# Which of two sequences goes first: the sample through projections, attention and recurrence before the prompt, and the feed-forward begun with the sample

## The chip, the cores and the metric

The kernel runs on one core of one Trainium2 chip. TensorE (PE in the rows) multiplies matrices into PSUM banks, VectorE (DVE), ScalarE (ACT) and GpSimd (POOL) do the elementwise work, and every DMA is issued from SyncE's queue (SP). The metric is the device time of one execution in microseconds (us), as a median over runs. For one execution there is a profile: start and duration of each instruction, and what ended each wait.

## The reference

One encoder layer is applied to two token sequences with the same weights: the prompt ("p", 512 tokens) and the sample ("s", 1024 tokens), 1024 features each.

```python
mod = (jax.nn.silu(c) @ w_ada + b_ada)[:, None, :]
sh1, sc1, g1, sh2, sc2, g2 = jnp.split(mod, N_MOD, axis=-1)
n = rms_norm(x, ln1_g) * (1 + sc1) + sh1
z = n @ w_in
q, k, v, xl, gl = jnp.split(z, [D_ATT, 2 * D_ATT, 3 * D_ATT, 3 * D_ATT + D_LRU], axis=-1)
...
att = neighbourhood_attention(q, k, v, rpb)
xl = depthwise_conv(xl, lru_conv_w, lru_conv_b)
h = (rg_lru_direction(xl, w_r_f, b_r_f, w_i_f, b_i_f, lam_f, False)
     + rg_lru_direction(xl, w_r_b, b_r_b, w_i_b, b_i_b, lam_b, True))
lru = (h * jax.nn.gelu(gl.astype(jnp.float32))).astype(x.dtype)
mix = jnp.concatenate([att, lru], axis=-1) @ w_out
x = x + g1 * mix
n2 = rms_norm(x, ln2_g) * (1 + sc2) + sh2
up = depthwise_conv(n2 @ w_up, ffn_conv_w, ffn_conv_b)
ug, uv = jnp.split(up, 2, axis=-1)
x = x + g2 * ((jax.nn.gelu(ug) * uv) @ w_down)
```

The feed-forward is 1024 to 2 x 2816 and back, in 22 blocks h of 128 hidden features. Everything is fp32. A product is made as three matmuls of rounded parts (hi x hi, hi x lo, lo x hi), so each operand is first split into two parts by elementwise instructions.

## The kernel before, in words

The program is written as a list of operations: `Recorder.op` notes each operation's cost estimate, what it reads and writes, and its buffers, and issues nothing. `Recorder.run` then makes a plan on the host. It gives each operation a due time (from the place in the list and from what depends on it) and goes through the engines in the order of that plan, with room in two SBUF arenas (F and R, whose border moves at each `turn`) and eight PSUM banks as conditions. Operations with two possible engines (a split's copy on ACT or DVE, a difference on DVE or POOL) get theirs there. The result is one fixed order of instructions for each engine. On the chip each engine follows its order, and waits for what the next instruction needs.

Where the plan leaves PE without work for over 900 ns it puts in filler, matmuls of the identity into an empty bank (`spin`), 128 columns wide in fp32. They are made in two passes, and so have two records each in the trace. The rule is:

```python
IDLE, SHARE = 900.0, 0.6
...
            if e == "PE" and s - done > IDLE:

                k = int(SHARE * (s - done) / 221.0)
                ...
                    events.append(lambda k=k, at=min(free, key=lambda x: emptied[x]): self.spin(at, k))
```

Filler is executed whether or not PE would have to wait there on the chip.

The stages, in the order of the list before the change:

- Start: four chunks of the modulation matrix, the prompt's first norm, weights.
- For j = 0 to 3 the prompt's heads 2j and 2j+1 and one quarter of the recurrence (`proj`: `qkv`, `mod_chunk`, `lru`), then the same for the sample (j = 3 to 0). Beside each `proj`, `weave` puts the attention (`attend`) of the step ahead of it. The sample's norm stands ahead of its first `proj`.
- The last attention (sample, j = 0) goes beside the loading of w_out and the prompt's output projection (`out_proj`), which leaves x2 = x + g1 * mix in DRAM.
- The sample's two output projections of 512 tokens, beside the second norm (`norm2`) of the prompt and of the sample's first half. `norm2` reads x2 back, normalizes and transposes it, and `a_terms` makes from its quarter blocks 11, 12, 21, 22 the four sums s1 to s4 and splits all: the seven left operands of a Strassen-Winograd product, which has seven products in place of eight (`WINO`).
- The first four feed-forward blocks for the prompt alone, as plain products (eight quarter products, `plain=True`), beside `norm2` of the sample's second half. Then blocks 4 to 21 for both by the seven products, and blocks 0 to 3 for the sample.
- The down projection, again by seven products (`DOWN`), reads the hidden features back from DRAM, in pairs of blocks, and ends with the last product over three groups of tiles.

In the rows, L376 is the emitting line that all recorded operations share, L497 the transposes and L323 the filler. Buffers appear by arena, not by purpose: arena_f and pieceNF are fp32 room, arena_r and pieceNR room for split operands.

Of the kernel before, what the change touches and what calls it, by code (L numbers as in the profile page):

```python
# [32 lines left out]
STEPS = (140, 134, 160, 176, 186, 96, 124)  # L33
# [13 lines left out]
ONLY_P = 4  # L47

BOOST = 2e4
# [785 lines left out]
def encoder(ctx: ExitStack, tc: tile.TileContext, x_p, x_s, c_t, ada, bada, bgate, lng, w_qkv, w_xg,  # L835
# [371 lines left out]

    def chain(*gens):
        for g in gens:
            for _ in g:  # L1210
                yield 1
            yield 1
# [51 lines left out]
    def norm2(q, g, xt):  # L1264
        norm_scale(xt)
        yield 1
        if q == "p":
            for f in (0, 2):
# [11 lines left out]
                if ONLY_P:  # L1280
                    keep("21", halved(full["21"], "n2x", None, [P, 2, 256]))
# [33 lines left out]
    xt = norm1_load("p", 0)  # L1315
    wq0, wx0, wg0 = [], [], []
    for ci in range(4):
# [14 lines left out]
        for f in (2 * ci, 2 * ci + 1):  # L1332
            norm_feature("p", 0, 1, xt, n1["p"], f)
# [28 lines left out]
    prev = w3 = wxg3 = None  # L1362

    for n, (q, j) in enumerate([("p", j) for j in range(4)] + [("s", j) for j in (3, 2, 1, 0)] + [("d", 0)]):
        out = []
        if q == "d":
            R.turn(1)
            main, nmain = chain(load_wo(), out_proj("p", [0])), 2
        else:
            if (q, j) == ("p", 3):  # L1370
                w3, wxg3 = load_w(w_qkv[j], 384), [load_w(w_xg[i + j], P) for i in (0, 4)]
            w, wxg = (wq0, (wx0, wg0)) if n == 0 else (w3, wxg3) if j == 3 else (None, None)
            main, nmain = proj(q, j, n + 4, out, w, wxg, n == 0), 6 if q == "p" else 13
            if n == 4:
                main, nmain = chain(norm_all("s"), main), 61
        if prev is None:
            weave(main, nmain, None, 1)
        else:
            pq, pj, pk = prev
            weave(main, nmain, attend(pq, pj, pk), 7 if pq == "p" else 15)  # L1380
        prev = (q, j, out[0]) if out else None
# [9 lines left out]

    R.turn(2)
    weave(out_proj("s", [0]), 4, norm2_of("p", 0), 2)
    R.turn(3)
    weave(out_proj("s", [1]), 8, norm2_of("s", 0), 7)
# [19 lines left out]
    def up(h, qs, plain=False):  # L1415
# [33 lines left out]
        if plain:  # L1449
            w = {k: halved(full[k], "wu", None) for k in ("11", "21", "12", "22")}  # L1450
            for q in qs:
                th = seqs[q]["T"] // 2
                for n in range(2):
                    pt = R.bank("up")
                    for m in range(2):
# [38 lines left out]
    def ups(hs, qs, plain):  # L1494
        for h in hs:
            up(h, qs, plain)
            if h == ONLY_P - 1:
                R.turn(4)
# [226 lines left out]
```

## Time and profile before

| | us |
|---|---|
| median of 2 runs | 1711.74 (1709.38 to 1714.09) |
| the profiled execution | 1708.56 |
| span of its instructions | 1706.8 |
| PE busy | 1664.3 (98%) |
| PE weight loads (PEld) | 1419.9 (83%) |
| DVE, ACT, POOL busy | 1344.4, 826.0, 550.8 |

The profiled execution lies 3.2 us below the median, and its span 1.8 us below its own time. A busy PE counts the filler as work, and its matmuls overlap, so that two neighbours that each last 0.39 us start 0.23 us apart. What PE loses in a stretch is therefore read as its idle time there plus the busy time of the filler.

### The profile page before, as it was taken

The numbers are of one execution on the slowest core, as the hardware profiler recorded it, in microseconds if no ns is written. First come the engines' busy times: TensorE is split into PE (matmuls) and PEld (weight loads), VectorE is DVE, ScalarE is ACT, GpSimd is POOL, SyncE is SP. The second block draws the span as 40 slices with busy tenths as digits, with TensorE's granted clock in tenths as the row PEclk, the third lists the DMA queues.
The fourth block names the chain that finished last, engine by engine and source line by source line (L and its number), as shares of the span: only waits on it lengthen the run. The fifth ranks groups of instructions, "written<-read, shape, count | busy, mean of one in ns | idle before, by whom it ended". The sixth has DMA issues, their size and how long they took to land.

```text
span 1706.8 us, 25295 instructions
## 1 busy us (share of the span) xinstructions
PE 1664.3 (98%) x9098; PEld 1419.9 (83%) x9098; DVE 1344.4 (79%) x2501; ACT 826.0 (48%) x1433; POOL 550.8 (32%) x344
## 2 busy tenths in 40 slices
PE   8999899999998999999999999999999999999898
PEld 6888697879886888998888888888888888888687
DVE  6898986978799957687777767677778777987896
ACT  3678955767877724554343333334346432232130
POOL 0242220211226205173322222222136210595593
PEclk9999999999998999999999999999999999999999
DMA  9665242524356383631321121212122478657861
GB/s 368 238 219 179 75 166 81 207 84 157 134 199 236 115 264 121 231 118 38 93 66 59 56 75 56 73 52 81 46 76 90 134 249 304 236 178 241 274 219 62
DMA packets 130477, 253.90 MB, mean 149 GB/s; under 512 B 13600, under 2 KB 45984, under 8 KB 130352
## 3 DMA queue, kind: packets, MB, share of 16 engines
q1 hardware_dynamic: 130352, 252.29, 44.1%
q8 instruction: 71, 1.16, 0.3%
q14 instruction: 54, 0.44, 0.1%
HBM read 207.66 MB, written 44.58 MB: 148 GB/s over the span
## 4 chain that ended last, share of the span: by engine, by line
PE 69%; DVE 9%; DMA 6%; ACT 6%; POOL 5%; issue 4%; SPq 1%; DVEq 0%; ACTq 0%; POOLq 0%
PE bank L376 67%; DVE arena_f L376 2%; POOL arena_r L376 2%; PE bank L497 2%; DVE arena_r L376 2%; ACT arena_f L376 2%; ACT piece3F L376 1%; DVE piece3F L376 1%; DVE piece4F L376 1%; ACT L376 1%; POOL arena_f L376 1%; SPq L376 1%; DMA piece3F<-in_ada_dram 1%; DMA piece4F<-in_gatew_dram 1%; ACT piece4F L376 1%
## 5 line engine op out<-in xcount | busy, mean ns | idle before, releaser
L376 PE MATMUL bank<-arena_r 128*128 128x512 f32 (+3 forms) x2700 | 653.6, 366 | 10.7 <-DVE piece4F L376 4.1
L376 PEld LDWEIGHTS bank<-arena_r 128*128 128x128 f32 (+1 forms) x2700 | 480.9, 189 | 90.3 <-DVE piece4F L376 5.0
L376 POOL TENSOR_TENSOR arena_f<-arena_f 128x512 f32<-128x512 f32 (+1 forms) x83 | 117.1, 1413 | 366.5 <-DMA arena_f<-in_w_up_dram 115.3
L376 PE MATMUL bank<-arena_r,piece5R 128*128 128x256 f32 (+1 forms) x1028 | 227.9, 323 | 2.3 <-DVE arena_f L376 1.1
L376 PE MATMUL bank<-piece0R,arena_r 128*128 128x512 f32 (+2 forms) x683 | 210.2, 391 | 2.1 <-ACT piece3F L376 1.4
L376 PEld LDWEIGHTS bank<-arena_r,piece5R 128*128 128x128 f32 x1028 | 168.5, 189 | 23.1 <-DVE piece5R L376 2.1
L376 PE MATMUL bank<-arena_r,piece0R 128*128 128x384 f32 (+3 forms) x750 | 179.3, 345 | 2.8 <-DVE piece0R L376 2.0
L376 DVE SCALAR_TENSOR_TENSOR arena_f<-bank,arena_s,arena_f 128x511 f32<-128x511 f32 (+3 forms) x306 | 153.8, 534 | 23.1 <-ACT arena_f L376 16.0
L376 PE MATMUL bank<-arena_r,piece3R 128*128 128x256 f32 (+1 forms) x686 | 163.1, 328 | 1.1 <-DVE bank L376 0.7
L376 ACT ACTIVATE arena_f<-arena_f,arena_s 128x384 f32<-128x384 f32 (+3 forms) x183 | 110.9, 616 | 95.1 <-DVE arena_f L376 65.6
L376 POOL TENSOR_TENSOR arena_r<-arena_f,arena_r 128x768 fp32r<-128x768 f32 (+2 forms) x60 | 100.3, 1681 | 154.2 <-ACT arena_r L376 53.4
L376 PEld LDWEIGHTS bank<-piece0R,arena_r 128*128 128x128 f32 (+1 forms) x683 | 123.1, 188 | 29.6 <-ACT piece3F L376 2.4
L376 PEld LDWEIGHTS bank<-arena_r,piece0R 128*128 128x128 f32 (+1 forms) x750 | 129.8, 189 | 13.6 <-issue 4.4
L376 ACT ACTIVATE arena_f<-bank 128x512 f32<-128x512 f32 (+2 forms) x149 | 69.2, 470 | 137.2 <-DVE bank L376 77.3
L376 ACT ACTIVATE arena_f<-bank,arena_s 128x512 f32<-128x512 f32 (+1 forms) x134 | 91.2, 689 | 84.5 <-PE bank L376 62.4
L376 PEld LDWEIGHTS bank<-arena_r,piece3R 128*128 128x128 f32 x686 | 116.2, 189 | 15.3 <-DVE bank L376 0.9
L376 ACT ACTIVATE arena_r<-arena_f 128x768 fp32r<-128x768 f32 (+3 forms) x97 | 69.2, 720 | 86.6 <-PE bank L376 43.9
L376 DVE TENSOR_TENSOR arena_r<-arena_f,arena_r 128x768 fp32r<-128x768 f32 (+2 forms) x79 | 84.2, 1074 | 5.8 <-ACT arena_r L376 4.7
L376 DVE TENSOR_TENSOR arena_f<-arena_f 128x512 f32<-128x512 f32 (+2 forms) x78 | 73.3, 950 | 13.6 <-ACT arena_f L376 12.5
L376 ACT ACT_TABLE_LOAD x53 | 68.0, 1283 | 11.1 <-issue 4.7
L376 PE MATMUL bank<-piece0R,piece3R 128*128 128x512 f32 (+1 forms) x227 | 69.0, 373 | 0.0
L376 DVE TENSOR_TENSOR bank<-bank,arena_f 128x512 f32<-128x512 f32 (+1 forms) x80 | 46.1, 576 | 25.5 <-PE bank L376 14.1
(454 smaller groups left out, 3131.8 us busy)
## 6 DMA issues: line engine op xcount, KB each, us to landing
arena_f<-in_w_up_dram SPq DMA_DIRECT2D x98, 256.0 KB, 3.5
arena_f<-gd SPq DMA_DIRECT2D x55, 384.0 KB, 3.8
gd<-arena_f SPq DMA_DIRECT2D x62, 256.0 KB, 3.3
arena_f<-in_bias_s_dram SPq DMA_DIRECT2D x31, 384.0 KB, 5.5
arena_f<-in_w_qkv_dram SPq DMA_DIRECT2D x28, 384.0 KB, 5.4
piece4F<-in_ada_dram SPq DMA_DIRECT2D x18, 512.0 KB, 9.0
piece3F<-in_ada_dram SPq DMA_DIRECT2D x16, 512.0 KB, 8.1
piece1F<-in_w_down_dram SPq DMA_DIRECT2D x31, 256.0 KB, 5.1
```

The lines of the kernel that those rows point to most:

```text
L376: fn(**{k: (v.real() if isinstance(v, View) else v) for k, v in kw.items()})
L497: self.op("PE", 107.0, lambda: self.nc.tensor.transpose(out.real(), in_.real(), ident.real()), [in_, ident], [out])
```

## The change

The sample now goes through the first norm, the projections, attention and the recurrence ahead of the prompt. The second half of its tokens is normalized right ahead of the loop. The prompt follows (j = 3 to 0). w_out is loaded beside the second of the prompt's steps. The sample's first output projection goes beside the prompt's last `proj`, its second one and `norm2` of its first half beside the prompt's last attention. Then come the prompt's output projection beside `norm2` of the sample's second half, the first two feed-forward blocks (h = 0, 1) for the sample alone by the seven products, beside `norm2` of the prompt, then blocks 2 to 21 for both, and blocks 0 and 1 for the prompt. The plain form is gone, and so is the extra split term that it needed. The borders of the arenas (`STEPS`) and one constant of the due times (`BOOST`) have other values. `mixed` interleaves two parts in a given proportion.

```diff
-STEPS = (140, 134, 160, 176, 186, 96, 124)
+STEPS = (146, 160, 174, 172, 182, 98, 130)
...
-ONLY_P = 4
-
-BOOST = 2e4
+ONLY = 2
+WO = 5
+
+BOOST = 16e3
...
+    def mixed(a, na, b, nb):
+
+        i = j = 0
+        while a is not None or b is not None:
+            if b is None or (a is not None and i * nb <= j * na):
+                i += 1
+                if next(a, 0) == 0:
+                    a = None
+                    continue
+            else:
+                j += 1
+                if next(b, 0) == 0:
+                    b = None
+                    continue
+            yield 1
...
-                if ONLY_P:
-                    keep("21", halved(full["21"], "n2x", None, [P, 2, 256]))
...
-    xt = norm1_load("p", 0)
+    xt = norm1_load("s", 0)
...
-            norm_feature("p", 0, 1, xt, n1["p"], f)
+            norm_feature("s", 0, 1, xt, n1["s"], f)
...
-    for n, (q, j) in enumerate([("p", j) for j in range(4)] + [("s", j) for j in (3, 2, 1, 0)] + [("d", 0)]):
-        out = []
-        if q == "d":
-            R.turn(1)
-            main, nmain = chain(load_wo(), out_proj("p", [0])), 2
-        else:
-            if (q, j) == ("p", 3):
...
+    norm_group("s", 1, 1, norm1_load("s", 1), n1["s"])
+
+    for n, (q, j) in enumerate([("s", j) for j in range(4)] + [("p", j) for j in (3, 2, 1, 0)] + [("d", 0)]):
+        out = []
+        if q == "d":
+            R.turn(1)
+            main, nmain = mixed(out_proj("s", [1]), 4, norm2_of("s", 0), 10), 14
+        else:
+            if (q, j) == ("s", 3):
...
+            if n == 4:
+                main, nmain = chain(norm_all("p"), main), 9
+            elif n == WO:
+                main, nmain = chain(load_wo(), main), 15
+            elif n == 7:
+                main, nmain = mixed(main, 6, out_proj("s", [0]), 4), 10
...
     R.turn(2)
-    weave(out_proj("s", [0]), 4, norm2_of("p", 0), 2)
+    weave(out_proj("p", [0]), 4, norm2_of("s", 1), 6)
     R.turn(3)
-    weave(out_proj("s", [1]), 8, norm2_of("s", 0), 7)
...
-    weave(ups(range(ONLY_P), ["p"], True), max(ONLY_P, 1), norm2_of("s", 1), 6)
+    weave(ups(range(ONLY), ["s"]), 7 * ONLY, norm2_of("p", 0), 4)
     R.turn(4)
...
-    for h in range(ONLY_P, NH):
-        up(h, ["p", "s"])
-    for h in range(ONLY_P):
-        up(h, ["s"])
+    for h in range(ONLY, NH):
+        for _ in up(h, ["p", "s"]):
+            pass
+    for h in range(ONLY):
+        for _ in up(h, ["p"]):
+            pass
...
-    pairs = list(range(ONLY_P // 2, NH // 2)) + list(range(ONLY_P // 2))
+    pairs = list(range(ONLY // 2, NH // 2)) + list(range(ONLY // 2))
```

Counted over both programs, PE has 2248 matmuls of 256 columns before and 2200 after. Those of 384 and of 512 columns are as many as before (1344 and 4482). Of 128 columns there are 652 and 820: the 544 transposes stay, and filler goes from 108 matmuls in 11 runs to 276 in 21 runs. The first run, at the start of the program, has 33 in both. After the change 42 stand in the eight runs from the prompt's first norm to its last projection, and 201 in the twelve runs from the prompt's output projection on. In the program the lines are shifted by one: L324, L377 and L498.

The first place is PE's order behind the transposes of `norm2` of the sample's second half. Before, the plain products of the prompt follow (256 columns wide, moving operand 256):

```order
L497 MATMUL bank_72<-ident,arena_f 128x128 x4
L323 MATMUL bank_67<-ident 128x128 x21
L376 MATMUL bank_74<-arena_r,piece0R 128x256 x12
L376 MATMUL bank_74<-piece3R 128x256 x6
L376 MATMUL bank_74<-arena_r,piece3R 128x256 x6
```

After, the third and the fourth tile of the prompt's output projection follow there (512 columns wide, two banks of 24 matmuls a tile):

```order
L498 MATMUL bank_73<-ident,arena_f 128x128
L498 MATMUL bank_73<-ident,piece5F 128x128
L324 MATMUL bank_72<-ident 128x128 x19
L377 MATMUL bank_74<-piece0R 128x512
...
L377 MATMUL bank_67<-arena_r,piece0R 128x512 x15
L324 MATMUL bank_72<-ident 128x128 x54
L377 MATMUL bank_74<-piece0R,arena_r 128x512
L377 MATMUL bank_74<-piece1R,arena_r 128x512
```

One run of 21 became two of 19 and 54, and 48 matmuls of 512 columns stand between them.

The second place is PE's order where `norm2` of the sequence that comes last is made: the sample's before, beside block 4 (and before it the plain products), the prompt's after, beside block 1. Before:

```order
L376 MATMUL bank_69<-piece1R,arena_r 128x512 x3
L323 MATMUL bank_67<-ident 128x128 x6
L376 MATMUL bank_68<-arena_r,piece5R 128x256 x7
...
L376 MATMUL bank_69<-piece0R,arena_r 128x512
L323 MATMUL bank_71<-ident 128x128 x8
L376 MATMUL bank_68<-arena_r,piece5R 128x256 x12
```

After, where block 1 is made for the sample alone:

```order
L377 MATMUL bank_71<-arena_r 128x512 x9
L324 MATMUL bank_69<-ident 128x128 x48
L377 MATMUL bank_71<-piece3R,arena_r 128x512 x3
L377 MATMUL bank_71<-piece0R,arena_r 128x512 x3
L377 MATMUL bank_71<-arena_r 128x512 x6
L324 MATMUL bank_69<-ident 128x128 x6
L377 MATMUL bank_74<-arena_r 128x512 x9
L377 MATMUL bank_74<-piece0R,arena_r 128x512 x3
L324 MATMUL bank_69<-ident 128x128 x10
```

Each of the last three products of block 1 (12 matmuls) has a run of filler ahead of it, of 48, 6 and 10, and a run of 18 follows ahead of block 2.

The third place is DVE's order around the split of the output projection's tiles. Before, the split's difference for the third tile of the sample's second half (1024 elements, into piece3R) stands between the evictions of the third and of the fourth tile of its first half, so that three tiles of matmuls lie ahead of the ones that need it:

```order
L376 TENSOR_TENSOR piece4F<-bank_74,arena_f 128x512
L376 TENSOR_TENSOR piece4F<-bank_73,arena_f 128x512
L376 TENSOR_TENSOR piece4F<-piece4F 128x1024
L376 TENSOR_TENSOR piece3R<-arena_f,piece3R 128x1024
L376 TENSOR_TENSOR piece4F<-bank_74,arena_f 128x512
```

After, for the prompt's fourth tile, the split's difference (the last row) stands behind the evictions of the third tile (the first three rows) and instructions of the sample's `a_terms`, so that none of the output projection's matmuls lie ahead any more:

```order
L377 TENSOR_TENSOR arena_f<-bank_74,arena_f 128x512
L377 TENSOR_TENSOR arena_f<-bank_67,arena_f 128x512
L377 TENSOR_TENSOR arena_f<-arena_f 128x1024
L377 TENSOR_TENSOR arena_f<-arena_f 128x512
L377 TENSOR_TENSOR piece0R<-arena_f,piece0R 128x512
L377 TENSOR_TENSOR arena_f<-arena_f 128x512
L377 TENSOR_TENSOR arena_r<-arena_f,arena_r 128x512
L377 TENSOR_TENSOR arena_f<-arena_f 128x512
L377 TENSOR_TENSOR arena_r<-arena_f,arena_r 128x512 x2
L377 TENSOR_TENSOR arena_f<-arena_f 128x512
L377 TENSOR_TENSOR arena_r<-arena_f,arena_r 128x512
L377 TENSOR_TENSOR arena_r<-arena_f,arena_r 128x1024
```

From the difference for the third tile to that for the fourth, DVE's order has in all 9 differences and 6 sums of 512 elements, the two evictions, the sum of 1024 elements, and the difference for the fourth tile itself.

## Rows read from the trace of the kernel before

**Rows 1.** The page: busy us, share of the span and records of each engine

```profile
PE 1664.3 (98%) x9098; PEld 1419.9 (83%) x9098; DVE 1344.4 (79%) x2501; ACT 826.0 (48%) x1433; POOL 550.8 (32%) x344
```

**Rows 2.** Stretches: length, busy PE, PEld, DVE, ACT, POOL, PE's granted clock, DMA, GB/s

```profile
0.00:60.00 60.00, 55.70 (x334) 40.79 (x335) 39.38 (x128) 23.68 (x39) 2.80 (x8) 0.97 0.95 360
180.00:240.00 60.00, 53.98 (x339) 47.86 (x337) 52.69 (x143) 44.31 (x79) 20.04 (x14) 0.97 0.27 91
525.00:560.00 35.00, 28.93 (x136) 21.35 (x135) 33.20 (x51) 32.28 (x49) 27.99 (x10) 0.80 0.57 190
715.00:760.00 45.00, 43.02 (x365) 42.82 (x364) 36.31 (x49) 25.19 (x40) 24.19 (x16) 1.00 0.44 139
780.00:830.00 50.00, 48.13 (x281) 41.82 (x280) 34.99 (x60) 18.85 (x33) 12.27 (x9) 1.00 0.17 48
```

**Rows 3.** The same stretches, busy PE and PEld of the filler (L323) alone

```profile
0.00:60.00 60.00, 10.02 (x66) 9.82 (x66) 0.97 0.95 360
180.00:240.00 60.00, 8.38 (x66) 7.96 (x66) 0.97 0.27 91
525.00:560.00 35.00, 2.08 (x8) 1.78 (x8) 0.80 0.57 190
715.00:760.00 45.00, 5.68 (x48) 5.53 (x48) 1.00 0.44 139
780.00:830.00 50.00, 3.44 (x28) 3.43 (x28) 1.00 0.17 48
```

**Rows 4.** The filler's run of 21 by itself

```profile
733.00:738.00 5.00, 4.78 (x42) 4.77 (x42) 1.00 0.71 188
```

**Rows 5.** Stretches of the feed-forward: up for both, its end, down, down's last product

```profile
830.00:1300.00 470.00, 469.90 (x2687) 412.70 (x2687) 352.19 (x649) 185.64 (x321) 113.80 (x84) 1.00 0.22 67
1300.00:1380.00 80.00, 78.25 (x341) 63.25 (x340) 61.78 (x95) 42.06 (x66) 33.33 (x23) 1.00 0.43 135
1380.00:1600.00 220.00, 220.00 (x972) 182.16 (x971) 176.73 (x197) 54.90 (x78) 98.16 (x56) 1.00 0.73 247
1600.00:1625.00 25.00, 18.96 (x72) 13.95 (x71) 23.27 (x20) 3.91 (x5) 25.00 (x14) 0.93 0.72 243
```

**Rows 6.** PE in order of time, 703 to 741: start, us, instruction, idle before

```profile
703.42 0.39 PE L376 MATMUL bank<-piece0R,arena_r 128*128 128x512 f32 x1
...
721.81 2.32 PE L376 MATMUL bank<-arena_r,piece4R 128*128 128x256 f32 x18
723.97 1.60 PE L376 MATMUL bank<-arena_r,piece3R 128*128 128x256 f32 x12
...
730.05 3.33 PE L497 MATMUL bank<-ident,arena_f 128*128 128x128 f32 x29
733.22 4.85 PE L323 MATMUL bank<-ident 128*128 128x128 f32 x42
...
740.29 1.46 PE L376 MATMUL bank<-arena_r,piece0R 128*128 128x256 f32 x10 [1.98 <-DVE piece0R L376]
```

**Rows 7.** POOL in order of time, 733 to 780: the first and the last

```profile
733.03 1.52 POOL L376 TENSOR_TENSOR arena_f<-arena_f 128x512 f32<-128x512 f32 x1 [44.00 <-PE bank L497]
...
778.21 1.67 POOL L376 TENSOR_TENSOR arena_r<-arena_f,arena_r 128x512 fp32r<-128x512 f32 x1 [2.25 <-DVE arena_r L376]
```

**Rows 8.** The stretches of `a_terms`: the sample's second half, the prompt

```profile
729.00:780.00 51.00, 49.02 (x374) 46.96 (x373) 46.76 (x42) 29.44 (x51) 41.81 (x26) 1.00 0.40 119
655.00:684.00 29.00, 29.00 (x146) 24.48 (x145) 27.38 (x21) 16.01 (x27) 23.69 (x14) 1.00 0.44 142
```

**Rows 9.** DVE's groups of one shape, whole span: busy us, mean ns, idle before

```profile
L376 DVE TENSOR_TENSOR arena_f<-arena_f 128x512 f32<-128x512 f32 x74 | 68.0, 930 | 13.2 <-ACT arena_f L376 12.5 <-POOL arena_f L376 0.6
L376 DVE TENSOR_TENSOR arena_r<-arena_f,arena_r 128x512 fp32r<-128x512 f32 x26 | 29.9, 1156 | 2.4 <-ACT arena_r L376 2.1
L376 DVE TENSOR_TENSOR arena_f<-bank,arena_f 128x512 f32<-128x512 f32 x26 | 17.8, 685 | 3.6 <-PE bank L376 3.5
```

**Rows 10.** DVE's groups in the stretch 520 to 800, 1024 elements

```profile
L376 DVE TENSOR_TENSOR arena_r<-arena_f,arena_r 128x1024 fp32r<-128x1024 f32 x2 | 2.4, 1220 | 0.8 <-ACT arena_r L376 0.8
```

More of the change, by code (lines that the diff above doesn't have):

```diff
@@ L1360, in encoder @@
     R.ts(spn8, acc, -8.0, None, ALU.mult)
-    prev = w3 = wxg3 = None
-    for n, (q, j) in enumerate([("p", j) for j in range(4)] + [("s", j) for j in (3, 2, 1, 0)] + [("d", 0)]):
-        out = []
-        if q == "d":
-            R.turn(1)
-            main, nmain = chain(load_wo(), out_proj("p", [0])), 2
-        else:
-            if (q, j) == ("p", 3):
[L1371 to L1381, printed above, removed]
     def norm2_of(q, g):
@@ L1390, in norm2_of @@
         yield from norm2(q, g, xt)
+    prev = w3 = wxg3 = None
+    norm_group("s", 1, 1, norm1_load("s", 1), n1["s"])
[6 more added lines that the diff above has]
+            if (q, j) == ("s", 3):
+                w3, wxg3 = load_w(w_qkv[j], 384), [load_w(w_xg[i + j], P) for i in (0, 4)]
+            w, wxg = (wq0, (wx0, wg0)) if n == 0 else (w3, wxg3) if j == 3 else (None, None)
+            main, nmain = proj(q, j, n + 4, out, w, wxg, n == 0), 6 if q == "p" else 13
+            if n == 4:
[4 more added lines that the diff above has]
+                main, nmain = mixed(main, 6, out_proj("s", [0]), 4), 10
+        if prev is None:
+            weave(main, nmain, None, 1)
+        else:
+            pq, pj, pk = prev
+            weave(main, nmain, attend(pq, pj, pk), 7 if pq == "p" else 15)
+        prev = (q, j, out[0]) if out else None
     R.turn(2)
-    weave(out_proj("s", [0]), 4, norm2_of("p", 0), 2)
+    weave(out_proj("p", [0]), 4, norm2_of("s", 1), 6)
     R.turn(3)
-    weave(out_proj("s", [1]), 8, norm2_of("s", 0), 7)
     def wu_blocks(h):
@@ L1413, in encoder, with up @@
     off = {"p": 0, "s": TP}
-    def up(h, qs, plain=False):
+    def up(h, qs):
         full = wu_blocks(h)
@@ L1447, in finish @@
                 R.dma(g_d[h, :, off[q] + i * 512:off[q] + i * 512 + 512], cu)
[L1449 to L1455, printed above, removed]
-                        sts = [tuple(v[:, k * P:k * P + P] for v in w["12"[kk] + "12"[n]]) for kk in range(2) for k in range(4)]
-                        R.mm3(pt[:, m * th:m * th + th], sts, [n2[q]["12"[m] + "12"[kk], k] for kk in range(2) for k in range(4)])
-                    centre(q, n, 0, pt)
-                    side(q, n, 0, pt)
-                finish(q)
-            return
         for name, ka, kb, bank, first in WINO:
@@ L1492, in up, with ups @@
                     finish(q)
-    def ups(hs, qs, plain):
+            yield 1
+    def ups(hs, qs):
         for h in hs:
-            up(h, qs, plain)
-            if h == ONLY_P - 1:
-                R.turn(4)
-            yield 1
-    weave(ups(range(ONLY_P), ["p"], True), max(ONLY_P, 1), norm2_of("s", 1), 6)
+            yield from up(h, qs)
+    weave(ups(range(ONLY), ["s"]), 7 * ONLY, norm2_of("p", 0), 4)
     R.turn(4)
```

## The prediction

> **What bounds the kernel now.** I read the page first, then stretches, then the order of time on PE and POOL at the seam between attention and feed-forward. PE is busy for 98% of the span, and no other engine over 79% [rows 1]. So the time is PE's work plus what PE loses. In the up stage PE is busy for 469.90 of 470 us, and in most of the down stage for all of it [rows 5]; there only the number of matmuls counts. But a busy PE includes filler. In the first 60 us it executes 10.02 us of filler and idles 4.30. Four later stretches hold all the other filler [rows 2, 3], and what they lose, idle time and filler together, is:
>
> - 180 to 240 (from the prompt's to the sample's projections): 6.02 + 8.38 = 14.40 us, 33 filler matmuls;
> - 525 to 560 (end of attention): 6.07 + 2.08 = 8.15 us, 4 of them;
> - 715 to 760 (`norm2` of the sample's second half): 1.98 + 5.68 = 7.66 us, 24 of them;
> - 780 to 830 (the first blocks for both): 1.87 + 3.44 = 5.31 us, 14 of them.
>
> Together 35.52 us for 75. The change is decided by what it does to these losses, and by how many matmuls there are.
>
> **Matmuls.** 48 of 256 columns go: four plain blocks for the prompt were 4 x 96 = 384, and as seven products they are 4 x 84 = 336. Between 721.81 and 723.97, 18 such matmuls start [rows 6], 0.120 us each. 48 x 0.120 = 5.8 us less, all on the path. Transposes and wide matmuls stay. That two blocks of feed-forward instead of four are made for one sequence at a time moves DVE and ACT work about; in the up stage DVE is busy for 352 of 470 us [rows 5], and its cover remains. I cost it at nothing.
>
> **Filler.** The orders show 276 filler matmuls instead of 108, with the first 33 in both. Their own price: 21 of them keep PE busy for 4.78 us [rows 4], 0.228 each. They are executed in any case, so 243 later ones cost at least 55.3 us. They stand where PE's next instruction was expected late, so waits come on top. The four stretches give a price with the waits: 35.52 / 75 = 0.474 us for one filler matmul, from 12.97 / 38 = 0.341 (715 to 760 and 780 to 830, beside `norm2` and `a_terms`) to 14.40 / 33 = 0.436 (180 to 240, where a new sequence's norm is made). The stretch with only four is dominated by something else: its clock was granted at 0.80 on average [rows 2]. So the bounds are:
>
> - low: 243 x 0.228 = 55.3 us, 19.8 more than the 35.5 of now;
> - high: 243 x 0.474 = 115.1 us, 79.6 more.
>
> I take the nearest stretch for each. The 42 before the prompt's output projection are like 180 to 240: 42 x 0.436 = 18.3 us. The 201 behind it are like the two stretches beside `a_terms`: 201 x 0.341 = 68.6 us. Together 86.9, which is 51.4 more than now.
>
> **Does the seam really wait that long?** Two chains say that there is something to wait for. First, the sample's second half. Its `a_terms` begin on POOL at 733.03 and end at 779.88, POOL almost without a break [rows 7], with DVE busy for 46.76 of 51 us [rows 8]. That is 47 us. Before, PE had the prompt's plain products beside it, whose operands were all there. After, the list leaves two tiles of the prompt's output projection, 96 matmuls of 512 columns. 972 of these take 220.00 us [rows 5], 0.226 each, so 21.7 us, which leaves 25 us open. And the second of these tiles isn't ready: on DVE the difference for its split stands behind 9 differences and 6 sums of 512 elements, two evictions and one sum of 1024. By [rows 9, 10] these and the difference itself take 9 x 1.156 + 6 x 0.930 + 2 x 0.685 + 2 x 1.22 = 19.8 us, while PE has one tile, 48 x 0.226 = 10.9 us. PE is short of some 9 us there, and executes 54 filler matmuls, 12.3 us.
>
> Second, the prompt. From the last output matmul at 703.42 to the block of transposes at 730.05 it takes 26.6 us now (eviction, x2 to DRAM and back, squares, scaling) [rows 6], and the prompt's `a_terms` lie in a stretch of 29 us [rows 8]. So some 56 us pass from the prompt's last output matmul to its last operand. Beside it PE has blocks 0 and 1 for the sample: 168 x 0.226 = 38.0 us. 18 us stay open, and the splits of block 1's own weights stand in the same queues. Both chains together leave PE 43 us short, against 45.8 us (201 x 0.228) of filler there. That is without contention between the two chains, which share DVE, POOL and ACT, so it speaks for the low end or more, and not for less.
>
> On the other hand the Trainium skill, "Perfetto Trace Analysis", section Optimization Strategy, says that a kernel whose busiest engine changes over time may gain from interleaving such regimes. By that rule sample-first would gain, since it puts output projection and feed-forward of one sequence beside the norms of the other. The trace shows such interleaving already before (POOL and DVE above 80% beside a PE at 96%, [rows 8]), so it decides no term here; it is the reason for the first rival below, which has its time from rows alone.
>
> **Start.** In the first 60 us the DMA engines are busy for 0.95 of the time at 360 GB/s [rows 2]. SP's order now has the sample's other four x tiles (4 x 0.5 MB) ahead of the fifth chunk of the modulation, which is 2.1 MB / 360 GB/s = 5.8 us if nothing covers it, and nothing if the projections of the first half do. DVE has a second norm there, beside 39.38 us of work in 60. I take 3 us, from 0 to 6.
>
> **The rest.** The end of attention, which lost 8.15 us [rows 2, 3], is the prompt's after the change, with tiles of the sample's output projection and one norm beside it; its loss is in the 35.5 and in the new price alike. The tail of the up stage (1.75 us idle) becomes the prompt's alone, and the down stage's last product idles 6.04 us with POOL busy throughout [rows 5]; its pairs of blocks are only rotated by one instead of two. I leave both as they are, plus or minus 4 us.
>
> **Sum.** -5.8 + 51.4 + 3 = +48.6 us on the profiled execution's 1708.56: **1757 us**, 2.6% above the median of 1711.74. About 2% (34 us, so 1746) is what a measurement of this kernel tells from no change.
>
> **Rivals.**
>
> 1. *The filler only fills.* The waits are as long as the filler and no longer: each chain ends while it runs, since the chains' 43 us and the filler's 45.8 agree. The loss is 55.3 us: -5.8 + 19.8 + 3 = +17.0, **1726 us**, 0.8% above the median and so not slower by the bound. It decides if PE's idle time in the seam is below some 5 us in all. For it: the run of 21 is followed by a wait of only 1.98 us [rows 6]. Against it: filler covers only 0.6 of a gap by its own rule, and all four stretches show idle time beside it.
> 2. *The clock falls in the gaps.* At 525 to 560 PE waited several times and its granted clock was 0.80 on average, so part of that stretch ran at 1.2 instead of 2.4 GHz; the loss was 8.15 us for four filler matmuls [rows 2, 3]. Six runs of 15 to 54 with waits behind them could each do that. All at 0.474: -5.8 + 79.6 + 3 = +76.8, **1785 us**. The Trainium skill, "TensorE: Matmul & The Clock Gate", section "Why this matters for your kernels", says that gaps between bursts of matmuls put the array back to half rate. Stretch 525 to 560 agrees; stretches 715 to 760 and 780 to 830 held the clock (granted 1.00) with filler.
> 3. *A real gain.* Even where nothing is lost in the later stretches but the filler itself, 55.3 us of filler stand against 35.5 lost now. With all idle time of the start (4.30), of the up stage's tail (1.75) and of the down stage's last product (6.04) gone as well, it is 1708.6 - 5.8 + 19.8 - 12.1 = **1710 us**, the same time.
>
> That the sample is begun with is in the order, so "it does not do what it says" is no case.
>
> **How the numbers follow.** Forecast (waits as at the nearest stretches, 1757): 0.50. Filler only (1726): 0.27. Clock (1785): 0.18. A real gain or something else: 0.05. The range goes from the filler-only case to the clock case with the start's and the end's few us: 1722 to 1788. Faster by over 2% (below 1677): 0.01. Within 2%: the filler-only case, a small part of the forecast's, and most of the rest, 0.33. Slower by over 2%: 0.66.
>
> **What would show it.** 552 records of L324 and some 62 us of PE busy on them, of which 46 us behind the start of the prompt's output projection; PE's idle time beside the later filler some 32 us (86.9 less 55.3); the up stage still without idle time; 0 to 60 us much as before. The forecast is wrong at its root if PE's idle time falls in spite of the filler, for then the places of the filler say nothing on waits; it is mis-sized if idle time beside the filler is below 10 us or above 50, or if the start or the down stage differ by more than 10 us.

## The result, and the profile after

The kernel after takes 1771.88 us (median of 2 runs, 1770.01 to 1773.74) against 1711.74: 1.0351 times as long, 95% interval 1.0319 to 1.0383. The profiled execution took 1773.74 us, its span is 1772.0, which is 65.2 us more than before. The forecast of 1757 us was 15 us short, inside its range.

The page of the kernel after, its line of engines, beside [rows 1]:

```profile
PE 1711.7 (97%) x9386; PEld 1459.8 (82%) x9386; DVE 1383.3 (78%) x2548; ACT 842.1 (48%) x1452; POOL 539.4 (30%) x327
```

PE is busy for 47 us longer although, filler apart, it has 48 matmuls less. Stretches of the kernel after, columns as in [rows 2]; all engines:

```profile
0.00:60.00 60.00, 54.20 (x350) 40.06 (x351) 38.76 (x138) 30.34 (x50) 0.96 (x7) 0.97 0.78 301
180.00:520.00 340.00, 327.75 (x1961) 281.69 (x1960) 294.13 (x735) 271.76 (x499) 99.11 (x58) 0.98 0.49 169
520.00:640.00 120.00, 119.86 (x615) 98.66 (x614) 82.02 (x188) 65.15 (x122) 15.15 (x8) 1.00 0.55 187
640.00:900.00 260.00, 238.64 (x1328) 204.95 (x1327) 166.61 (x258) 90.95 (x150) 71.40 (x46) 0.95 0.28 91
900.00:1300.00 400.00, 397.48 (x2264) 347.68 (x2263) 309.40 (x565) 149.94 (x252) 73.26 (x53) 1.00 0.20 61
1620.00:1665.00 45.00, 34.79 (x129) 26.67 (x128) 41.07 (x38) 13.06 (x19) 24.19 (x13) 0.81 0.74 242
```

The same of its filler alone (L324 in this kernel; here the column after the length is PE's):

```profile
0.00:60.00 60.00, 9.04 (x66) 0.97 0.78 301
180.00:520.00 340.00, 12.86 (x84) 0.98 0.49 169
640.00:900.00 260.00, 46.91 (x402) 0.95 0.28 91
```

And 640 to 900 us in the kernel before, first all engines, then (L323) the filler:

```profile
640.00:900.00 260.00, 256.05 (x1562) 228.29 (x1561) 200.67 (x297) 116.99 (x195) 100.33 (x64) 1.00 0.35 111
640.00:900.00 260.00, 9.13 (x76) 1.00 0.35 111
```

In both kernels 640 to 900 us holds the seam: `norm2`, its `a_terms`, and the first blocks of the feed-forward. What PE loses there, idle time and filler together, is 3.95 + 9.13 = 13.1 us before and 21.36 + 46.91 = 68.3 after, 55.2 more. The start loses 14.8 (14.3 before), and 520 to 640 nothing, where the end of attention stood [rows 2, 3].

How the seam loses is seen where the largest burst of `a_terms` lies. Before, that of the sample's second half, in steps of 10 us:

```profile
740.00:750.00 10.00, 9.71 (x81) 9.71 (x82) 10.00 (x10) 5.31 (x9) 9.40 (x6) 1.00 0.54 144
750.00:760.00 10.00, 10.00 (x86) 10.00 (x85) 9.79 (x10) 4.90 (x8) 9.09 (x7) 1.00 0.47 156
760.00:770.00 10.00, 10.00 (x73) 9.42 (x72) 10.00 (x11) 5.38 (x11) 10.00 (x7) 1.00 0.18 61
770.00:780.00 10.00, 10.00 (x57) 8.73 (x56) 9.36 (x8) 4.95 (x11) 7.62 (x5) 1.00 0.38 107
```

After, that of the prompt:

```profile
760.00:770.00 10.00, 8.92 (x55) 7.61 (x54) 10.00 (x10) 8.15 (x15) 7.97 (x6) 1.00 0.46 136
770.00:780.00 10.00, 10.00 (x92) 10.00 (x91) 10.00 (x9) 5.16 (x9) 10.00 (x7) 1.00 0.56 150
780.00:790.00 10.00, 5.30 (x19) 3.88 (x18) 6.59 (x6) 1.52 (x3) 4.81 (x3) 0.83 0.24 74
790.00:800.00 10.00, 8.29 (x50) 6.67 (x49) 5.91 (x11) 1.59 (x2) 0.00 (x0) 0.98 0.01 2
```

Both have DVE and POOL at or near 10 of 10 us while the burst lasts. Before, PE has the prompt's plain quarters beside that. After, its work has run out, as PE in order of time shows (start, us, instruction, idle before); the rows of 699 and 714 are the same story at the sample's second half:

```profile
699.24 12.22 PE L324 MATMUL bank<-ident 128*128 128x128 f32 x108
714.60 0.80 PE L377 MATMUL bank<-piece0R,arena_r 128*128 128x512 f32 x1 [3.14 <-ACT arena_r L377]
...
769.73 10.88 PE L324 MATMUL bank<-ident 128*128 128x128 f32 x96
781.57 0.73 PE L377 MATMUL bank<-piece3R,arena_r 128*128 128x512 f32 x2 [0.96 <-ACT arena_r L377]
786.04 0.79 PE L377 MATMUL bank<-piece3R,arena_r 128*128 128x512 f32 x1 [3.74 <-DVE arena_r L377]
```

12 and 11 us of filler, each with waits for a split operand behind it. And as soon as the burst is over, POOL has nothing to do (0.00 in the row from 790, and in each 10 us up to 830): the elementwise work is not too much for the whole seam (DVE 166.61 of 260 us, less than before), it is too much at once.

### The profile page after: what moved, and what is told of

Its sections match the earlier page's. It is cut to its first block, busy times and chain, and to the rows that moved or that the text cites. A ratio compares the mean times of both kernels' runs of the same rounds, so it can differ in the third digit from the quotient of the medians.

```text
span 1772.0 us, 25907 instructions
## 1 busy us (share of the span) xinstructions
PE 1711.7 (97%) x9386; PEld 1459.8 (82%) x9386; DVE 1383.3 (78%) x2548; ACT 842.1 (48%) x1452; POOL 539.4 (30%) x327
## 4 chain that ended last, share of the span: by engine, by line
PE 51%; DVE 9%; DMA 2%; ACT 1%; issue 1%; POOL 1%; SPq 0%; ACTq 0%; DVEq 0%; POOLq 0%
PE bank L377 51%; DVE arena_f L377 4%; DVE arena_r L377 2%; ACT arena_f L377 1%; DVE piece5F L377 1%; DVE piece5R L377 1%; DMA arena_f<-catdp 0%; PE bank L498 0%; DMA x2ds<-arena_f 0%; DMA piece4F<-in_w_down_dram 0%; DVE piece4F L377 0%; POOL arena_r L377 0%; DVE piece0R L377 0%; DVE piece0F L377 0%; DVE piece2F L377 0%
## 5 line engine op out<-in xcount | busy, mean ns | idle before, releaser
L377 PE MATMUL bank<-arena_r 128*128 128x512 f32 (+2 forms) x2916 | 709.4, 371 | 13.2 <-POOL arena_r L377 5.3
L377 PEld LDWEIGHTS bank<-arena_r 128*128 128x128 f32 x2916 | 535.1, 190 | 103.8 <-POOL arena_r L377 6.8
L377 PE MATMUL bank<-arena_r,piece5R 128*128 128x256 f32 (+1 forms) x1311 | 269.2, 314 | 2.8 <-DVE piece5R L377 2.8
L377 POOL TENSOR_TENSOR arena_f<-arena_f 128x512 f32<-128x512 f32 (+1 forms) x83 | 124.7, 1503 | 431.6 <-DVE arena_f L377 169.6
L377 PEld LDWEIGHTS bank<-arena_r,piece5R 128*128 128x128 f32 x1311 | 212.6, 192 | 25.6 <-DVE piece5R L377 3.2
L377 PE MATMUL bank<-arena_r,piece0R 128*128 128x384 f32 (+3 forms) x793 | 182.7, 346 | 0.1
L377 DVE SCALAR_TENSOR_TENSOR arena_f<-bank,arena_s,arena_f 128x511 f32<-128x511 f32 (+3 forms) x320 | 159.5, 529 | 29.8 <-ACT arena_f L377 22.2
L377 ACT ACTIVATE arena_f<-arena_f,arena_s 128x384 f32<-128x384 f32 (+3 forms) x193 | 116.0, 614 | 99.0 <-DVE arena_f L377 69.1
L377 ACT ACTIVATE arena_f<-bank,arena_s 128x512 f32<-128x512 f32 (+2 forms) x160 | 108.1, 681 | 98.7 <-PE bank L377 66.3
L377 PE MATMUL bank<-piece0R,arena_r 128*128 128x512 f32 (+2 forms) x433 | 142.7, 396 | 4.8 <-ACT arena_r L377 3.1
L377 PEld LDWEIGHTS bank<-arena_r,piece0R 128*128 128x128 f32 (+1 forms) x793 | 134.1, 188 | 15.5 <-issue 3.4
L377 ACT ACTIVATE arena_f<-bank 128x512 f32<-128x512 f32 (+2 forms) x144 | 67.4, 472 | 156.8 <-DVE bank L377 71.7
L377 POOL TENSOR_TENSOR arena_r<-arena_f,arena_r 128x768 fp32r<-128x768 f32 (+3 forms) x68 | 117.1, 1733 | 63.0 <-ACT arena_r L377 57.5
L377 ACT ACTIVATE arena_r<-arena_f 128x768 fp32r<-128x768 f32 (+3 forms) x122 | 87.6, 736 | 98.9 <-PE bank L377 59.3
L377 PE MATMUL bank<-arena_r,piece1R 128*128 128x384 f32 (+3 forms) x456 | 106.6, 340 | 1.7 <-DVE arena_s L377 1.0
L377 DVE TENSOR_TENSOR arena_r<-arena_f,arena_r 128x768 fp32r<-128x768 f32 (+2 forms) x85 | 102.6, 1217 | 6.9 <-ACT arena_r L377 3.6
L377 PE MATMUL bank<-arena_r,piece4R 128*128 128x256 f32 (+1 forms) x463 | 107.3, 315 | 0.0
L377 PE MATMUL bank<-piece0R,piece5R 128*128 128x512 f32 x301 | 100.7, 401 | 2.8 <-DVE arena_f L377 2.8
L377 DVE TENSOR_TENSOR arena_f<-arena_f 128x512 f32<-128x512 f32 (+2 forms) x102 | 90.8, 907 | 14.7 <-ACT arena_f L377 6.6
L377 PEld LDWEIGHTS bank<-piece0R,arena_r 128*128 128x128 f32 (+1 forms) x433 | 79.2, 191 | 20.2 <-ACT arena_r L377 3.3
L377 PEld LDWEIGHTS bank<-arena_r,piece4R 128*128 128x128 f32 x463 | 79.5, 190 | 8.5
L377 PEld LDWEIGHTS bank<-arena_r,piece1R 128*128 128x128 f32 (+1 forms) x456 | 75.5, 189 | 11.2 <-DVE arena_s L377 3.0
```

Source lines behind the costliest of these rows:

```text
L377: fn(**{k: (v.real() if isinstance(v, View) else v) for k, v in kw.items()})
```

## The experiments

The theory after the traces: PE starves in the seam while DVE and POOL make operands of the seven products, and has lost the matmuls that covered this. Rivals: the filler itself costs the time; the sample-first order of the earlier stages does; a delay that no amount of elementwise work changes; the luck of one plan. For every run the time is the median, the ratio is to runs of the kernel before on the same chip, and the loss is PE's idle time plus filler of its profiled execution, in four stretches (in brackets PE's granted clock in the seam); "work" is PE's busy time without filler. The profiled execution of e5 is the slowest of its four, 7.6 us above their median.

| run | us | ratio to before, 95% | 0-60 | 60-640 | seam, 640-900 (clock) | 900-end | work |
|---|---|---|---|---|---|---|---|
| before | 1711.74 | | 14.3 | 31.7 | 13.1 (1.00) | 13.0 | 1634.7 |
| after | 1771.88 | 1.0319-1.0383 | 14.8 | 26.3 | 68.3 (0.95) | 19.7 | 1642.9 |
| e1 | 1779.59 | 1.0383-1.0423 | 13.9 | 19.9 | 61.8 (0.85) | 21.3 | 1659.7 |
| e2 | 1721.32 | 1.0043-1.0079 | 14.9 | 28.9 | 11.2 (0.97) | 12.9 | 1651.8 |
| e3 | 1717.66 | 1.0030-1.0057 | 14.1 | 34.3 | 27.6 (0.99) | 8.5 | 1631.0 |
| e4 | 1711.78 | 0.9990-1.0014 | 14.1 | 35.3 | 20.9 (1.00) | 13.8 | 1622.1 |
| e5 | 1784.72 | 1.0404-1.0455 | 14.7 | 41.0 | 64.0 (0.94) | 21.8 | 1649.0 |
| e6 | 1754.33 | 1.0225-1.0261 | 14.4 | 27.3 | 55.1 (0.96) | 16.3 | 1641.2 |
| e7 | 1714.59 | 1.0005-1.0028 | 14.2 | 31.5 | 6.7 (1.00) | 26.6 | 1631.2 |
| e8 | 1785.10 | 1.0408-1.0443 | 14.5 | 34.9 | 66.9 (0.97) | 28.0 | 1638.7 |
| e9 | 1775.26 | 1.0364-1.0398 | 14.4 | 41.2 | 41.6 (0.98) | 22.9 | 1651.7 |
| e10 | 1758.52 | 1.0264-1.0294 | 14.2 | 24.5 | 59.1 (0.97) | 22.4 | 1638.1 |
| e11 | 1744.61 | 1.0173-1.0241 | 14.3 | 44.0 | 13.1 (1.00) | 27.3 | 1640.8 |
| e12 | 1743.34 | 1.0172-1.0210 | 14.2 | 45.3 | 2.7 (1.00) | 33.2 | 1646.0 |

**e1 and e2: no filler behind the start.** The same edit in the kernel after (e1) and before (e2); the order of everything else stays.

```diff
-                k = int(SHARE * (s - done) / 221.0)
+                k = int((SHARE if done == 0.0 else 0.0) * (s - done) / 221.0)
```

> The changed kernel without any filler but the first run of 33; every other instruction in the same order. Theory A (the waits come from operands that are late, and filler runs inside them): PE's idle time takes the place of some 59 us of filler, and the time stays within 1.5% of the changed kernel's 1772, 1755 to 1795, perhaps later because the clock falls in longer gaps. Rival B (the filler itself holds up PE): the time falls by most of the extra filler's 38 us or more, to 1715 to 1735.

> The kernel before, without any filler but the first 33. Theory A: within 1% of 1712. Rival B: 1692, all 20 us of the later filler saved.

Both are slower and not faster, e1 by 8 us against the kernel after (their intervals just touch), e2 by 10 us against the kernel before; rival B falls. The seam of e1, and two of its pieces:

```profile
640.00:900.00 260.00, 198.16 (x886) 159.56 (x885) 158.80 (x246) 86.80 (x143) 66.75 (x44) 0.85 0.27 85
...
710.00:720.00 10.00, 3.57 (x8) 2.37 (x9) 8.67 (x7) 3.76 (x7) 7.36 (x5) 0.50 0.64 184
...
780.00:790.00 10.00, 2.34 (x5) 1.43 (x6) 9.43 (x7) 2.19 (x4) 7.65 (x5) 0.50 0.36 105
```

PE simply idles where it executed filler: 61.8 us in place of 68.3. The clock, though, falls to its lower level in these gaps (0.50 of the full speed): 0.85 is granted in the seam, and 0.968 over the whole span (0.984 with the filler). Over the span the same matmuls keep PE busy for 1659.7 - 1642.9 = 16.8 us longer. The filler is not the cost; it marks the waits and holds the clock. The Trainium skill, "TensorE: Matmul & The Clock Gate", section "Why this matters for your kernels", says that idle gaps between bursts of matmuls put the array back to its lower rate; e1 agrees.

**e3: sample first, but the seam as before.** The kernel before with sample and prompt exchanged in the start and in the loop of projections and attention; the sample's first output projection goes beside the last attention, and the prompt's and `norm2` of the sample's first half change places with it; the prompt's four plain blocks beside `norm2` of the sample's second half stay. The first three borders of the arenas are those of the change. Its core:

```diff
-    for n, (q, j) in enumerate([("p", j) for j in range(4)] + [("s", j) for j in (3, 2, 1, 0)] + [("d", 0)]):
+    for n, (q, j) in enumerate([("s", j) for j in range(4)] + [("p", j) for j in (3, 2, 1, 0)] + [("d", 0)]):
...
-    weave(out_proj("s", [0]), 4, norm2_of("p", 0), 2)
+    weave(out_proj("p", [0]), 4, norm2_of("s", 0), 7)
...
-    weave(out_proj("s", [1]), 8, norm2_of("s", 0), 7)
+    weave(out_proj("s", [1]), 8, norm2_of("p", 0), 2)
```

> The sample first through projections, attention and recurrence as in the change (load of w_out beside the prompt's second step as well), but then the order of before: first output projection of the sample beside the last attention, then the prompt's and the norm of the sample's first half, then the sample's second and the prompt's norm, then four plain blocks for the prompt beside the norm of the sample's second half. Theory A (the seam is what costs): 1720 to 1745, the seam of before plus some 12 to 17 us for the prompt's norm chain, which has only four tiles of output projection beside it. Rival C (the new order of the earlier stages costs): 1755 or more.

By its total it is 6 us slower, a little under the range of theory A. By the stretches, 0 to 640 us loses 48.4 us against 46.0 before, so the order of the earlier stages is nearly free. The seam loses 27.6, 14.5 more than before, as the expectation had it for the prompt's norm with only four tiles beside it. So the order within the seam has a price of its own even with the plain blocks kept, but it is not most of the 55.2.

**e4 and e7: no low parts of `norm2`'s operands.** In `a_terms`, in the kernel after (e4) and, as the control, before (e7). The low parts of the left operands are not computed, but for the sample's quarters 11 and 12, which are split elsewhere; the high parts stand in their place.

```diff
-                keep(k, halved(full[k], name, None, shape))
+                hi = R.buf(shape, F32R, name)
+                R.act(hi, full[k], AF.Copy, either=True)
+                keep(k, (hi, hi))
```

> The changed kernel, but a_terms makes no low parts of its sums and quarter blocks: the rounded part is used twice. It leaves out 34 of the differences of 512 elements that DVE and POOL make in the seam (some 45 us of their time at 1.2 to 1.7 us), and no matmul, DMA or transpose. Theory A in the form 'DVE, POOL and ACT cannot make the operands as fast as PE uses them': the later filler's loss halves, 1735 to 1752. Rival D (latency decides: the way of x2 through DRAM, the row of small instructions of the norm, a split that waits for room): 1758 to 1775.

> The control of e4: the kernel before with the same part left out (the low parts of the operands of the seven products are not made; the high parts are used twice). e4 took 60 us from the kernel after. Theory A (what e4 took is the change's own loss in the seam): before loses 35.5 us in its later stretches, of which the seam's part is 8.15 + 7.66 + 5.31 = 21 us, so at most 10 to 25 us are to be had here: 1686 to 1701. Rival G (leaving the low parts out is worth as much in every order, as through the up stage): 1651.

With 34 differences less the kernel after has the time of the kernel before, where theory A had expected half of the way. Its seam, all engines and then filler:

```profile
640.00:900.00 260.00, 253.15 (x1385) 216.87 (x1384) 191.43 (x297) 128.44 (x222) 100.71 (x69) 1.00 0.35 114
640.00:900.00 260.00, 14.02 (x116) 1.00 0.35 114
```

The loss there fell by 47.4 us, to 20.9, and the clock is back at 1.00. PE's work takes 20.8 us less, at 0.998 of the clock over the span. In the kernel before the same omission takes only 6.4 us out of the seam and the time doesn't fall at all, which both expectations missed: 900 to the end loses 13.6 us more, in another plan. So e4's gain is not that of leaving work out in any order. It is the change's own loss, and it hangs on elementwise work. The rival of a delay that this work doesn't set falls.

**e5: one part of the change alone.** The kernel before, its first four prompt blocks by seven products, without the split of quarter 21.

```diff
-                if ONLY_P:
-                    keep("21", halved(full["21"], "n2x", None, [P, 2, 256]))
...
-    weave(ups(range(ONLY_P), ["p"], True), max(ONLY_P, 1), norm2_of("s", 1), 6)
+    weave(ups(range(ONLY_P), ["p"], False), max(ONLY_P, 1), norm2_of("s", 1), 6)
```

> The kernel before, in its old order, with one part of the change alone: the prompt's first four blocks of feed-forward are made as seven products (and the extra split of quarter 21 goes) and not as four plain quarters. Theory A (the seam between attention and feed-forward is bound by elementwise work, and the plain form spared that work where it was scarce): 48 matmuls of 0.120 us go, 5.8 us, but the sums and splits of four blocks' weights and the sums of the prompt's norm2 now stand before the first products; slower than before by 5 to 30 us, so 1716 to 1741. Rival M (PE's work alone counts, and the seam's loss comes from the order): faster by the 5.8 us, about 1705. If it is slower by more than 30 us, the dropped plain form explains most of the change by itself.

The strongest single result: 73 us slower, as much as the whole change or more, with 5.8 us fewer matmuls to do. Its seam:

```profile
640.00:900.00 260.00, 235.90 (x1431) 210.78 (x1431) 172.44 (x273) 95.79 (x170) 82.13 (x51) 0.94 0.31 99
640.00:900.00 260.00, 39.92 (x336) 0.94 0.31 99
```

64.0 us in place of 13.1, in the old order and with the old borders and `BOOST`. The plain quarters, whose operands need no sums, were the cover. Beyond the 30 us named beforehand, this makes the dropped plain form the main cause. What the plain form gave was two things: matmuls whose operands were there, and less to prepare (e5 has 4365 instructions on DVE, ACT and POOL, the kernel before 4278). Their shares were not measured apart.

**e6 and e9: plain quarters in the kernel after,** for the sample's first two blocks (e6) and for four (e9); borders of the arenas moved to make room.

```diff
-STEPS = (146, 160, 174, 172, 182, 98, 130)
+STEPS = (146,160,176,176,182,98,130)
...
+                keep("21", halved(full["21"], "n2x", None))
...
-            yield from up(h, qs)
+            yield from up(h, qs, True)
```

with the plain form of `up` as in the kernel before, for 1024 tokens, and for e9 `ONLY = 4` and `STEPS = (146,160,178,178,182,98,130)`.

> The kernel after, with plain quarters for the sample's first two blocks again (quarter 21 of the sample's second half is split as well; the third to fifth boundary of the memory arenas are moved by 2 to 4 KiB, since it doesn't fit otherwise). The sample's plain product costs 4 x 48 matmuls of 512 columns and not 7 x 24 = 168, so 24 more each at 0.226 us: 2 x 24 x 0.226 = 10.8 us more of matmuls. Theory A (elementwise work bounds the seam): it is gained back or more, since PE has more work beside norm2 whose operands come with fewer sums and splits; 1750 to 1770 against 1772. Rival M (PE's work counts): 1783.

> The kernel after with four of the sample's blocks made alone and in plain quarters (e6 had two, and took 1754 in place of 1772). Two more plain sample blocks are 48 more matmuls of 512 columns, 10.8 us. Theory A (operands that need sums and splits are what the seam lacks; plain quarters need none of the sums): the loss that is left in e6 against the kernel before goes further, by more than the 10.8 us: 1735 to 1752. Rival M (two blocks were enough cover, the rest is PE's own work): 1765.

The seam's loss falls to 55.1 and 41.6, by 13.2 us for two blocks and 26.7 for four. Both expectations count the price of this wrongly: a plain block of the sample has 96 matmuls of 512 columns for 84, so 12 more and not 24. The traces have 4506 and 4530 of them where the kernel after has 4482, and 24 and 48 more cost 5.4 and 10.8 us at 0.226. So in the seam the plain blocks win more than they cost. e6 gained 17.5 us in all, as theory A had it. e9 lost that again, and some 3 us more, outside the seam (60 to 640: 41.2 against 27.3, 900 to the end 22.9 against 16.3) and in PE's work (1651.7 against 1641.2). Its total missed both expectations; in the seam theory A there held, since two more blocks win 13.5 us for 5.4. Plain quarters of the prompt cost 12 x 0.120 = 1.4 us per block and cover more. All of their operands are there before the sample's second half is normalized; half of the sample's quarters wait for just that half. That this is the reason is read from the code and not tested by itself.

**e10: no low parts of the weights** of the two blocks for the sample alone (left out: 14 differences).

```diff
-    def b_term(full, k, name):
+    def b_term(full, k, name, alone=False):
...
+        if alone:
+            hi = R.buf([P, 512], F32R, name)
+            R.act(hi, full[k], AF.Copy, either=True)
+            return hi, hi
         return halved(full[k], name, None)
...
-            w = b_term(full, kb, "wu")
+            w = b_term(full, kb, "wu", qs == ["s"])
```

> The kernel after, without the low parts of the weights of the two blocks that are made for the sample alone (7 per block, the high part is used twice): 14 differences of 512 elements less in the seam, all for the weights and none for norm2. e4 left out 34 differences of norm2's operands and gained 60 us, 1.8 us for each. Theory A1 (any elementwise work in the seam costs alike, its capacity is the bound): 14 x 1.8 = 25 us less, 1740 to 1755. Theory A2 (the chain from norm2 to the first products is the bound, and the weights' splits lie in its gaps): 1762 to 1775.

1758.5 lies between the two expectations. The seam lost 59.1, 9.2 less, or 0.66 us for each difference; e4 gave 47.4 / 34 = 1.39. So elementwise work counts by where it stands: about half as much for these weights as for the operands that the bursts consist of. That some weights are split in the lulls would explain it; no run shows that. Neither reading, all alike (A1) or only the chain from `norm2` (A2), holds alone.

**e8 and e11: another seed of the planner's noise,** in the kernel after and before. The edit is one number:

```diff
-NOISE, SEED = 500.0, 1
+NOISE, SEED = 500.0, 2
```

> The kernel after with another seed of the planner's noise: the same generators, another order of the elementwise work in detail (301 filler matmuls and not 276). Theory A (the seam lacks elementwise capacity for any order of the same generators): within 10 us of the kernel after, 1762 to 1782. Rival L (the loss is bad luck of one plan): below 1750, or above 1795.

> The kernel before with another seed of the planner's noise (128 filler matmuls and not 108), the control of e8. If the time before was a lucky plan and the change lost that luck (rival L): 1725 or more. If the old order gives its time for other plans too (theory A): 1703 to 1720.

e8 lies 3 us above theory A's range and 10 below rival L's. e11 was a surprise: 33 us for a seed. The rival of luck is right about the total: times of two plans of the same list differ by 13 (after) and 33 us (before). From one pair of these four plans to another the change costs 27 to 73 us. The rival is wrong about the seam. The seam of e11, all engines and filler:

```profile
640.00:900.00 260.00, 254.62 (x1530) 225.53 (x1529) 195.94 (x313) 110.14 (x181) 78.52 (x49) 1.00 0.35 111
640.00:900.00 260.00, 7.72 (x62) 1.00 0.35 111
```

5.38 + 7.72 = 13.1 us as in the kernel before, and 66.9 against 68.3 after. What the seed moves lies in the other stretches (60 to 640: 44.0 against 31.7; 900 to the end: 27.3 against 13.0). So experiments that make a new plan (all but e1 and e2) are read by the seam's column; their totals carry some 30 us of luck. The change itself did not lose that luck: outside the seam it loses 60.8 us against 59.0.

**e12: six plain blocks in the kernel before,** `ONLY_P = 6`, the part that the change removed made larger, and the one candidate to beat both.

> The kernel before with six of the prompt's blocks made alone and in plain quarters, not four: the part that the change took away, made larger. Two more plain blocks are 2 x 12 matmuls of 256 columns more, 2.9 us. Theory A (the plain blocks cover the seam, and four cover it already: idle time and filler at 640 to 900 us are 13.1 us in the kernel before and in e11 alike, 64.0 in e5 without plain blocks): the seam loses 8 to 15 us, so the time is the one before plus the 2.9 us, but for the luck of another plan outside the seam: 1708 to 1730. Rival V (four were too few): the seam's 13.1 us go nearly whole, 1702 or less, and this version beats both.

The seam all but vanishes as a loss, to 2.7 us:

```profile
640.00:900.00 260.00, 258.99 (x1608) 233.42 (x1607) 201.03 (x313) 111.89 (x182) 93.12 (x59) 1.00 0.39 124
640.00:900.00 260.00, 1.72 (x14) 1.00 0.39 124
```

There rival V was right, four blocks had not covered all. The total is 33 us worse, with 45.3 us lost in 60 to 640 and 33.2 behind 900, where the plan is another; both expectations missed it. In the old order the dose is clear, in one plan each: none, four and six plain blocks lose 64.0, 13.1 and 2.7 us in the seam. No version that ran beats the kernel before.

## Why the prediction was right or wrong

Term by term, forecast and what the two profiled executions show:

| term | forecast, us | measured, us |
|---|---|---|
| start, 0 to 60 | +3 | 14.3 to 14.8: +0.5 |
| from the first half to the end of attention (180 to 640) | 18.3 for 14.40 + 8.15: -4.2 | 29.9 to 25.2: -4.7 |
| the seam (640 to 900) | 68.6 for 12.97: +55.6 | 13.1 to 68.3: +55.2 |
| the rest (60 to 180, 900 to the end) | 0, plus or minus 4 | -0.7 and +6.7 |
| PE's own work | -5.8 | +8.2 |
| sum | +48.6 | +65.2 |

**Filler and waits: right in size.** 201 x 0.341 = 68.6 us was forecast for the seam, and 68.3 came, with 46.9 us of filler (46 forecast). Idle time from 60 to 900 is 13.4 + 21.4 = 34.8 us (32 forecast). The 552 records of filler came as forecast, with 68.8 us for some 62: the earlier ones were dearer than 0.228 each. The 21.4 us idle in the seam rule out rival 1, which allowed 5. The price is no accident of one plan: in the ten other kernels with filler in the seam, the loss there is 0.33 to 0.42 us for each filler matmul.

**But not for the reason given.** "They are executed in any case, so 243 later ones cost at least 55.3 us" is the step that e1 refutes: without them the kernel is no faster, but 8 us slower. The planner put them where it expected PE to wait, and PE does wait there, for 61.8 us in e1. They were a good measure of the waits and no cost. Rivals 1 and 3 took that price as their floor.

**Moved elementwise work "at nothing": wrong, and without harm to the sum.** That the change "moves DVE and ACT work about" was priced at nothing, and the cover for it was sought in the up stage. The cover that mattered went with the plain form: e5, without it alone, lost 64.0 us in the seam and not 13.1. The two chains of the section on the seam had this in them ("PE had the prompt's plain products beside it, whose operands were all there"), and both are where the trace after shows filler, 12.22 and 10.88 us. There the mechanism was right. The sum did not suffer, because the planner had put filler where this work makes PE late, and the filler's price carried it.

**The clock: the missing term.** The forecast left it to rival 2. PE's work was to fall by 5.8 us and rose by 8.2, so the same matmuls took 14.0 us longer. The granted clock is 0.95 in the seam (1.00 before) and 0.81 from 1620 to 1665, in the down stage's last product (0.96 in a stretch of the same length and place before, 1600 to 1645); the mean of the span is 0.984 against 0.993. Rival 2 had the mechanism, with another price: the loss for a filler matmul in the seam stayed at 68.3 / 201 = 0.340, as at the nearest stretches, and the clock's cost came on top, in the matmuls that follow the gaps. 55.2 - 4.7 + 14.0 - 5.8 is most of the 65.2.

**The rest: mis-sized.** 900 to the end was to stay within 4 us and lost 6.7 more, in the down stage's last product for the most part. The runs don't tell why. The seeds moved the same stretch by 8 to 14 us, so it may be no more than another plan.

**Luck.** A total moves by 13 and 33 us with the seed alone, so that 1757 came within 15 us of 1771.88 is in part luck. The seam's 55.2 us is not: the seeds moved that stretch by 0.0 and 1.4.

**The rule on regimes.** That interleaving regimes may improve a kernel (the Trainium skill, "Perfetto Trace Analysis", section Optimization Strategy) was left without weight in the forecast. In the seam (64.0, 13.1 and 2.7 us lost) e5 and e12 agree with the rule and point to its condition here: the interleaving that paid is that of operand making with matmuls whose operands were ready; the change put other stages beside one another and lost that.

## What to carry to other kernels

Before a cheaper form of a product replaces a plain one, look at what runs beside the plain one: work that needs no preparation is the cover for preparing the rest, and here 5.8 us fewer matmuls went with some 50 us more loss in the stretch they covered (e5). Where a planner fills PE's gaps, read its filler as a map of expected waits and take it out once to see whether it costs or helps. Where a new plan follows from any edit, run another seed of both kernels first, and compare stretches, since totals differed by 13 and 33 us here for a seed.

## What the runs showed of the hardware

DVE's difference of 512 elements depends on POOL. DVE in order of time in the kernel after, one difference inside the burst and one behind it:

```profile
778.61 1.75 DVE L377 TENSOR_TENSOR arena_r<-arena_f,arena_r 128x512 fp32r<-128x512 f32 x1
...
791.24 0.69 DVE L377 TENSOR_TENSOR arena_r<-arena_f,arena_r 128x512 fp32r<-128x512 f32 x1
```

POOL at the same time, one of its operations and its last:

```profile
778.10 1.71 POOL L377 TENSOR_TENSOR arena_f<-arena_f 128x512 f32<-128x512 f32 x1
...
783.79 1.65 POOL L377 TENSOR_TENSOR arena_f<-arena_f 128x512 f32<-128x512 f32 x1 [0.63 <-DVE arena_r L377]
```

The same operation takes 1.75 us beside a busy POOL and 0.69 beside an idle one. Of DVE's operations of this form (512 elements, both operands in SBUF) that the trace of 640 to 900 us lists singly, the 42 beside an idle POOL took 0.67 to 0.69 us; the 28 with POOL busy for over half of their time took 0.68 to 1.78, 1.39 on average. In these rows the two engines finish two operations in 1.75 us, in which DVE alone would finish 2.5: POOL's help in the bursts seems to help nothing. The mean of 1.156 us in [rows 9], used in the forecast, mixes both. The Trainium skill, "SBUF — State Buffer", section "SBUF: two separate sides", says that DVE and GpSimd share a pair of ports that one of them holds for a whole instruction; the two durations agree. A plan that keeps POOL out of the bursts was not run, so what it would give stays open.
